# Two-layer hybrid encoder: layer B's output projection as two plain blocks of tokens and three pairs of blocks in seven half-size products

## The chip, the cores and the metric

The kernel runs on one core of a Trainium2 chip. The metric is device time in microseconds (us) of one execution. All matrix products are done on TensorE (PE); VectorE (DVE), ScalarE (ACT) and GpSimd (POOL) prepare operands and take results away; SyncE (SP) issues the DMAs in the order in which they stand in its program.

## What is computed

The reference is one step of an encoder with two attention layers over 2,048 prompt tokens and 64 sample tokens, 2,112 in all, with D_MODEL = 1024:

```
y_p = x_p + (op * jax.nn.silu(gp)) @ w_out
...
y_s = x_s + (os_ * jax.nn.silu(gs)) @ w_out
```

`op` and `os_` are the outputs of the attention of a layer (layer A: sliding window, grouped queries; layer B: 16 heads over the own chunk and 8 chunks before it), `gp` and `gs` the gates, and `w_out` is 1024 x 1024. The case is about this last product of layer B: gated attention (1024 features x 2,112 tokens, the DRAM tensor "ogb") times `w_out_b`, plus the residual x, gives the kernel's y.

## The kernel before

**Numbers and layout.** Activations stand feature-major: 128 partitions x 8 groups of features x 2,112 tokens. Every 32-bit operand of layer B's matmuls is split into two fp16 parts, hi and lo. ACT writes hi by a scaled activation, DVE then writes lo = scaled value - hi by a SCALAR_TENSOR_TENSOR. A product of a 128-row slice of features takes three matmuls: weights hi by x hi, weights hi by x lo, weights lo by x hi. One matmul has a 128 x 128 weight tile and 264 columns of tokens (OT = 2,112 / 8).

**Stages.** Layer A's projections and attention run first, then its output projection, then layer B's projections and attention, head pair by head pair (`hp` 0 to 7), then layer B's output projection. PE's order is written out by hand. While attention runs, a `Filler` (L1029) fills PE between score and value products with the next stage's matmuls, three at a step (L1039); `goal` (L1950) and `due` (L1920) say how many steps to place after each score product. The last head pair's attention is filled with layer B's output projection in this way. What is left of it runs alone at the end. The instructions of the other engines are put into an order by a scheduler; each engine then executes its own in that order, and waits where an operand or a buffer isn't ready.

**Layer B's output projection before** (`output_jobs(1, half, ..)`, L2010). Two halves of the 1024 output features, one after the other; in each half 8 blocks of 264 tokens; in each block 4 output tiles of 128 features; in each tile 8 groups of input features of three matmuls (L2051 to L2053). So 24 matmuls add up in one of two PSUM banks "pj", then one DVE instruction, the combine (L2057), adds bank x scale to a residual tile "res" that a DMA has loaded (L2016). Of every two output tiles a pair is stored (L2069). That makes 64 combines and 1,536 matmuls.

- `load_act` (L576) fetches a block's x in four DMAs of 264 KB (tag "xraw", XB = 4 buffers, L615) and splits each by ACT (L627) and DVE (L628) into "xx" (XN = 7 buffers). As the halves run one after the other, each block is loaded and split twice: 64 loads, 64 splits.
- `load_weights` (L493) loads a half's weights in eight pieces of 128 x 512 and splits each by ACT (L529) and DVE (L530). A half has its own eight, 16 in all.
- `Background` (L428) holds such splits back and places them by a budget: `drain` (L471), `share` (L485).
- POOL has no work in this stage; during the attention it makes the low parts of the softmax values (L1735) and multiplies outputs by gates (L1495).

In attention the instructions that appear in rows of the prediction are the score matmuls (L1678, L1679), the exponential on ACT (L1694) and the query split on DVE (L1633).

## Time and profile before

| | |
|---|---|
| three runs | 2070.81, 2071.38, 2074.5 us; median 2071.38 us |
| profiled execution | span 2081.5 us (the page gives no other time of it) |
| PE | busy 1994.4 us, 96% of the span |
| DVE, ACT, POOL | 68%, 69%, 54% of the span |
| granted PE clock | 9 (90% or more) in each of 40 slices |
| DMA | mean 206 GB/s; 429.11 MB |

In rows of a timeline the first number is the start in us from the span's start, the second the busy time in us; then engine, line, operation, output<-inputs, shape, and "xN" if N neighbouring instructions are drawn as one. In square brackets stands how long the engine stood idle before it and what released it. A row of windows gives from:to, length, then busy us (instructions) of PE, PE's weight load, DVE, ACT and POOL, the granted clock, the DMA share and GB/s. A row of groups gives the line, engine, operation and shape, the count, the busy us in all, the mean ns of one, and the idle time before with its releaser. A row of DMA issues gives count, KB each and the us from issue to landing.

### The profile page before, as it was taken

Reading aid. Unit: us, or ns where it says so; the run is one execution under the profiler, and the core shown is the slowest. Engines: PE = TensorE matmul, PEld = TensorE weight load, DVE = VectorE, ACT = ScalarE, POOL = GpSimd, SP = SyncE. Lnnn points to the kernel's source line nnn. Section 1 sums busy time; section 2 is a strip of 40 time slices with the busy share of each in tenths; the row PEclk is TensorE's granted clock in tenths of the full one; section 3 lists DMA queues with packets and bytes.
Section 4 is the critical chain, followed back from the end, with each engine's and each line's share of the span. In section 5 each row is a group of like instructions: output and inputs, shape, how many; then the busy total and the mean of one; then the engine's idle time right before and its main releaser. Section 6 shows DMA issues by size and latency. Waiting matters only on the chain.

```text
span 2081.5 us, 40775 instructions
## 1 busy us (share of the span) xinstructions
PE 1994.4 (96%) x12814; PEld 1429.3 (69%) x12814; DVE 1405.7 (68%) x4073; ACT 1439.1 (69%) x3572; POOL 1133.0 (54%) x1529
## 2 busy tenths in 40 slices
PE   7898999999999999989999999999999999999999
PEld 6777788777888999745555555555555555557888
DVE  7666777767667555677767676676766767667542
ACT  6777888777788433367778677787877778687430
POOL 5665565454447445578556565665756656565000
PEclk9999999999999999999999999999999999999999
DMA  8878787899766666789889789797987979678763
GB/s 259 252 209 220 218 213 184 228 232 240 210 159 177 197 215 204 265 227 248 218 184 244 167 200 222 175 238 176 201 221 171 245 163 215 154 155 200 229 198 113
DMA packets 610712, 429.11 MB, mean 206 GB/s; under 512 B 404208, under 2 KB 547968, under 8 KB 610464
## 3 DMA queue, kind: packets, MB, share of 16 engines
q1 hardware_dynamic: 610496, 426.51, 79.9%
q8 instruction: 101, 1.65, 0.3%
q14 instruction: 115, 0.94, 0.1%
HBM read 257.59 MB, written 73.43 MB: 159 GB/s over the span
## 4 chain that ended last, share of the span: by engine, by line
PE 54%; DVE 8%; ACT 6%; DMA 5%; issue 4%; POOL 2%; SPq 1%; ACTq 0%; DVEq 0%; POOLq 0%
PE pj L753 9%; PE pj L755 9%; PE pj L754 9%; PE o L1840 4%; PE pj L2051 4%; PE pj L2053 4%; PE pj L2052 4%; PE sb L1678 2%; PE sb L1679 2%; PE tp L1006 1%; DMA pt<-values 1%; DVE p L1682 1%; DVE wh L540 1%; DMA wraw<-in_w_o_a_dram 1%; POOL xx L635 1%
## 5 line engine op out<-in xcount | busy, mean ns | idle before, releaser
L753 PE MATMUL pj<-wh,xx 128*128 128x512 f16 (+2 forms) x1648 | 642.5, 390 | 22.4 <-DVE pa L847 9.6
L755 PE MATMUL pj<-wh,xx 128*128 128x512 f16 (+2 forms) x1648 | 624.0, 379 | 0.6 <-POOL xx L635 0.6
L1735 POOL TENSOR_TENSOR values<-p,values 128x640 f16<-128x640 f32 (+4 forms) x256 | 327.3, 1279 | 205.5 <-ACT values L1734 199.1
L754 PE MATMUL pj<-wh,xx 128*128 128x512 f16 x1024 | 388.3, 379 | 1.3 <-DVE wh L540 1.3
L1694 ACT ACTIVATE p<-p,nm 128x640 f32<-128x640 f32 (+5 forms) x264 | 199.5, 756 | 180.0 <-DVE nm L1687 141.0
L2051 PE MATMUL pj<-xx,wh 128*128 128x264 f32 (+1 forms) x1024 | 290.5, 284 | 11.2 <-DVE res L2057 4.0
L1682 DVE CUSTOM_DVE_ANT_0 p<-sb,BT 128x640 f32<-128x640 f32 (+5 forms) x272 | 196.5, 722 | 150.2 <-PE sb L1679 129.3
L2052 PE MATMUL pj<-xx,wh 128*128 128x264 f32 (+1 forms) x1024 | 287.6, 281 | 0.0
L635 POOL TENSOR_TENSOR xx<-xraw,xx 128x528 fp32r<-128x528 f32 (+4 forms) x144 | 184.7, 1304 | 100.2 <-ACT xx L634 92.9
L754 PE MATMUL pj<-wl,xx 128*128 128x512 f32 (+1 forms) x624 | 235.4, 377 | 2.4 <-DVE wl L540 2.4
L844 POOL TENSOR_TENSOR f<-f,mhalf 128x4 f32<-128x4 f32 x182 | 186.3, 1024 | 12.2
L755 PEld LDWEIGHTS <-xx 128*128 128x128 f16 x1024 | 100.2, 98 | 123.7 <-issue 1.9
L1342 ACT ACTIVATE p<-p,nm 128x257 f32<-128x257 f32 (+2 forms) x272 | 134.4, 496 | 70.5 <-DVE nm L1331 35.8
L1495 POOL TENSOR_TENSOR o<-gt,o 128x256 f32<-128x256 f32 (+1 forms) x132 | 104.9, 794 | 142.2 <-ACT p L1342 72.0
L1734 ACT CAST values<-p 128x640 f16<-128x640 f32 (+4 forms) x256 | 168.2, 658 | 12.5 <-DMA pt<-values 6.5
L754 PEld LDWEIGHTS <-xx 128*128 128x128 f16 x1024 | 100.3, 98 | 83.5 <-issue 3.6
L753 PEld LDWEIGHTS <-xx 128*128 128x128 f16 x1024 | 100.3, 98 | 82.0 <-ACT sq L822 1.4
L1840 PEld LDWEIGHTS <-values 128*128 128x128 f16 x1344 | 123.3, 98 | 38.8 <-DMA pt<-values 2.7
L753 PEld LDWEIGHTS pj<-wh,xx 128*128 128x128 f32 x624 | 119.7, 192 | 40.3 <-issue 8.1
L2053 PE MATMUL pj<-xx,wl 128*128 128x264 f32 x512 | 145.8, 285 | 0.9 <-DVE wl L533 0.9
L1840 PE MATMUL o<-pt,values 128*128 128x256 f16 (+1 forms) x1344 | 143.7, 255 | 1.7 <-DMA pt<-values 1.3
L2053 PE MATMUL pj<-xx,wh 128*128 128x264 f16 x512 | 141.3, 276 | 1.4 <-DVE wh L530 1.4
(292 smaller groups left out, 4719.8 us busy)
## 6 DMA issues: line engine op xcount, KB each, us to landing
xx<-xsb SPq DMA_DIRECT2D x112, 512.0 KB, 4.3
xx<-xsa SPq DMA_DIRECT2D x88, 512.0 KB, 5.0
xraw<-oga SPq DMA_DIRECT2D x64, 264.0 KB, 3.6
xraw<-ogb SPq DMA_DIRECT2D x64, 264.0 KB, 4.0
xsa<-xx SPq DMA_DIRECT2D x32, 512.0 KB, 4.0
wl<-in_w_in_b_dram SPq DMA_DIRECT2D x64, 256.0 KB, 4.9
wraw<-in_w_in_b_dram SPq DMA_DIRECT2D x56, 256.0 KB, 3.5
xraw<-in_x_dram SPq DMA_DIRECT2D x40, 256.0 KB, 4.6
```

The source lines that it names most:

```text
L635: nc.gpsimd.tensor_tensor(lo, rv, wide(hi), op=ALU.subtract)
L753: nc.tensor.matmul(ps[:n, :C], xh, wh, start=k == 0, stop=False)
L754: nc.tensor.matmul(ps[:n, :C], xh, wl, start=False, stop=False)
L755: nc.tensor.matmul(ps[:n, :C], xl, wh, start=False, stop=k == KC - 1)
L844: nc.gpsimd.tensor_tensor(fv, fv, mhalf[:n, :H], op=ALU.pow)
L1682: mi = nc.vector.tensor_tensor_reduce(out=p[r, :nk], in0=S[r, o : o + nk], in1=b, op0=ALU.add, op1=ALU.min, scale=1.0, scalar=3e38, accum_ ...
L1694: ex = nc.scalar.activation(p[:n, :nk], p[:n, :nk], AF.Exp, scale=-1.0, bias=it.nm[:n, c : c + 1], accum_out=it.sm[:n, c : c + 1],)
L1735: lo = nc.gpsimd.tensor_tensor(two[:, :, 1, :], pv, two[:, :, 0, :], op=ALU.subtract)
L1840: nc.tensor.matmul(it.O[:, h * T + q0 : h * T + q1_], held["VH"][:, kt, h], x, start=kt == kb and not low, stop=kt == tb and low == 1,)
L2051: nc.tensor.matmul(ps[:, :OT], wh, oh, start=k == 0, stop=False)
L2052: nc.tensor.matmul(ps[:, :OT], wh, ol, start=False, stop=False)
L2053: nc.tensor.matmul(ps[:, :OT], wl, oh, start=False, stop=k == KC - 1)
```

## The change

The two `output_jobs(1, ..)` give way to `fast_output_jobs(x1, y)`. The 2,112 tokens are taken as two single blocks of 264 ("spans" 0 and 1), then three pairs of blocks (528 tokens, spans 2 to 4).

A **single block** is computed as before, but for all 1024 output features in one pass: 8 output tiles of 24 matmuls and a combine. Two blocks have 384 matmuls and 16 combines.

A **pair** is computed by Strassen's scheme in Winograd's form, which takes 2 x 2 blocks: the two halves of the input features, the two halves of the output features, the two blocks of tokens. It has four groups, m = 0 to 3, one for each 128 features of an output half. A group takes seven products of half the depth: 4 groups of input features x 3 matmuls = 12 matmuls each. The products alternate between two fixed PSUM banks, whose sums run on from product to product, and after each product a combine (L2284 of the kernel after) adds the bank as it then stands to one quarter of the group's residual tiles ("res" for the upper output half, "more" for the lower). Three pairs have 3 x 4 x 7 x 12 = 1,008 matmuls and 84 combines.

**Operands of a pair.** The seven x operands are the raw quarters 0, 1, 2, 3, with four of them used as they are and three made from differences. POOL makes the differences in place in "xraw" (four subtractions of 128 x 528 a half, L2243); then ACT and DVE split each operand (L2192, L2195). It is done in two halves, e = 0 and 1, as "xraw" has four buffers and four quarters fill them: the loads of e = 1 stand behind the splits of e = 0 that read those buffers. So a pair has 8 loads, 14 splits and 8 subtractions. Each operand is a `Step`; a `drip` runs the next step, `force` runs what a product needs and isn't made. `operand(i + 1)` is called while span i runs, so that a pair's operands are made while the span before it is multiplied. Pair 1 and pair 3 lie in "xx", "ph", "pl", pair 2 in "values", "pt", "xx", tiles that the attention used.

**Weights.** `w_o_b` lies in another order in DRAM. There are 16 plain pieces and 16 mixed ones (sums and differences of pieces, by POOL, L2153, 16 operations of 128 x 512); all 32 are split once (ACT L2130, DVE L2131) and kept to the end. They are prepared by drips from step 8 of the last head pair on: one or two in each `due`, and after combines.

So there are 1,392 matmuls for 1,536, 100 combines for 64, 50 splits of x for 64, 40 loads of x for 64, 32 splits of weights for 16 with 32 loads for 16, and 40 POOL operations more. The scales of the splits change from 8 and WB_ to OO = 2 and WO = 2^12, and "ph" and "pl" hold 4 x 256 numbers for 5 x 256.

```diff
-        for half in range(2):
-            output_jobs(1, half, x1, y)
+        fast_output_jobs(x1, y)
...
+        spans = [(0, 1), (1, 1)] + [(2 + 2 * p, 2) for p in range(3)]
...
+        elif at == 8:
+            while held["chain"]:
+                held["chain"].pop(0)()
+            held["prepare"]()
...
                 if at:
                     bg.share(BL, BP_, KC)
+                    drip(1 + (len(drips["x"]) > 0))
...
+    def drip(n=1):
+        for _ in range(n):
+            for chain in drips.values():
+                if chain:
+                    chain[0].run()
+                    break
...
+    def force(*steps):
+        for x in steps:
+            while x.fn is not None:
+                drips[x.kind][0].run()
...
+            def s1():
+                for b in (2, 3, 0):
+                    raws[b] = raw_w(m, b)
+                return pool(3, 2, 3, ALU.add)
...
+        def split_x(dst, raw, guard):
+            hi, lo = (dst[:, :, q] for q in range(2))
+            r = nc.scalar.activation(hi, raw, AF.Identity, scale=S_OG)
...
+            nc.vector.scalar_tensor_tensor(lo, raw, S_OG, hi, op0=ALU.mult, op1=ALU.subtract)
...
+            def split(y_, k, at, less=()):
+                def part(e):
+                    if k == 0 and e:
+                        fetch_half(e)
...
+                    for o, a, b in less:
+                        nc.gpsimd.tensor_tensor(raws[e, o], raws[e, a], raws[e, b], op=ALU.subtract)
+                    split_x(x.parts[y_][:, 2 * e : 2 * e + 2], raws[e, at], tag in ("ph", "pl") and e == 0)
...
+            todo = [
+                split(0, 0, 0),
+                split(1, 1, 2),
+                split(2, 2, 3),
+                split(6, 3, 3, ((0, 1, 0), (1, 3, 1), (3, 3, 0))),
+                split(3, 4, 0),
+                split(4, 5, 1),
+                split(5, 6, 2, ((2, 2, 3),)),
+            ]
...
+        def product(w, x, xi, acc, start, stop=True):
+            force(w, *x.steps[xi])
+            for k in range(4):
...
+                combine(acc, rv[:, e])
+                if not filler.attending:
+                    drip(2)
...
+            for y_, (acc, wi, xi, start, rv) in enumerate((
+                (a, 0, 0, True, top[:, :OT]), (b, 1, 1, True, top[:, :OT]),
+                (a, 5, 6, False, top[:, OT:]), (b, 4, 3, True, bottom[:, OT:]),
+                (a, 6, 4, False, bottom[:, OT:]), (b, 2, 2, False, top[:, OT:]),
+                (a, 3, 5, False, bottom[:, :OT]),
+            )):
+                yield from product(ws[wi], x, xi, acc, start)
+                combine(acc, rv)
+                if not filler.attending and (y_ % 2 or m == 3):
+                    drip()
+                if wi == 2:
+                    store(xout[:, m, rows], top)
+                    next_res(i, m)
...
+                    if ready(i + 1) and (i or m == 4):
+                        st.x[i + 1] = operand(i + 1)
+                    yield from (group if n == 2 else alone)(i, x, m)
```

How instructions stand on DVE in the part that runs alone: before, in the second half of the output features. A combine (L2057) names its "res" tile and its bank "pj"; a split (L628) names its "xx" tile and the "xraw" buffer that it reads.

```order
L2057 SCALAR_TENSOR_TENSOR res_4986_26423<-pj_4988_26451,scl_90,res_4986_26423 128x264
L628 SCALAR_TENSOR_TENSOR xx_5008_26631<-xraw_5004_26612,scl_90,xx_5008_26631 128x528
L628 SCALAR_TENSOR_TENSOR xx_5024_26762<-xraw_5018_26748,scl_90,xx_5024_26762 128x528
L628 SCALAR_TENSOR_TENSOR xx_5024_26762<-xraw_5019_26750,scl_90,xx_5024_26762 128x528
L2057 SCALAR_TENSOR_TENSOR res_4993_26486<-pj_4994_26488,scl_90,res_4993_26486 128x264
L2057 SCALAR_TENSOR_TENSOR res_4993_26486<-pj_4997_26524,scl_90,res_4993_26486 128x264
L2057 SCALAR_TENSOR_TENSOR res_4998_26551<-pj_4999_26553,scl_90,res_4998_26551 128x264
```

And after, at the end of the first pair's group m = 0 and in m = 1. The combine is L2284, the split of an x operand L2195 (of 128 x 2 x 264), the split of a piece of weights L2131; "pj_4982" and "pj_4983" are the two banks.

```order
L2195 SCALAR_TENSOR_TENSOR xx_4996_26494<-xraw_4985_26287,scl_90,xx_4996_26494 128x2x264
L2284 SCALAR_TENSOR_TENSOR more_4974_26209<-pj_4982_26283,scl_90,more_4974_26209 128x264
L2131 SCALAR_TENSOR_TENSOR wl_5019_26701<-wraw_5016_26690,scl_90,wl_5019_26701 128x512
L2284 SCALAR_TENSOR_TENSOR res_4989_26379<-pj_4983_26284,scl_90,res_4989_26379 128x264
L2195 SCALAR_TENSOR_TENSOR pt_4991_26423<-xraw_4987_26291,scl_90,pt_4991_26423 128x2x264
L2195 SCALAR_TENSOR_TENSOR pt_4993_26459<-xraw_4984_26285,scl_90,pt_4993_26459 128x2x264
L2284 SCALAR_TENSOR_TENSOR res_4989_26379<-pj_4982_26283,scl_90,res_4989_26379 128x264
L2195 SCALAR_TENSOR_TENSOR xx_4999_26542<-xraw_4986_26289,scl_90,xx_4999_26542 128x2x264
L2195 SCALAR_TENSOR_TENSOR values_4988_26319<-xraw_5006_26590,scl_90,values_4988_26319 128x2x264
L2284 SCALAR_TENSOR_TENSOR res_4989_26379<-pj_4983_26284,scl_90,res_4989_26379 128x264
```

Before, two or three splits stand together between combines of 24 matmuls each; after, one or two stand between combines of 12 matmuls each. The buffer "xraw_5006" holds a quarter of the second half of pair 2's x. Its load goes into the room of "xraw_4985" and waits for that buffer's last reader, the split in the first row; its own split is the last but one row, ahead of the combine in the last row. From the first row to the last there are four combines, so four products.

On POOL before, the last instructions are those of the attention (o1 is a gated output, L1495 and L1805; "values" the low parts, L1735), and nothing follows them:

```order
L1495 TENSOR_TENSOR o1_4917_25852<-gt_4916_25850,o1_4917_25852 128x256
L1805 TENSOR_TENSOR o1_4929_25922<-G_4887_25614,o1_4929_25922 128x64
L1719 TENSOR_TENSOR G_4934_25974<-pb_4815_25160,sm_4899_25713 128x128 x2
L1735 TENSOR_TENSOR values_2366_11787<-p_4925_25882,values_2366_11787 128x5x128
L1495 TENSOR_TENSOR o1_4950_26113<-gt_4949_26111,o1_4950_26113 128x256
```

After, POOL goes on through the first pair with the differences of pair 2's quarters (L2243) and the mixed pieces of weights (L2153):

```order
L2243 TENSOR_TENSOR xraw_4984_26285<-xraw_4985_26287,xraw_4984_26285 128x528
L2153 TENSOR_TENSOR wraw_5015_26688<-wraw_5014_26686,wraw_5015_26688 128x512
L2153 TENSOR_TENSOR wraw_5014_26686<-wraw_5016_26690,wraw_5014_26686 128x512
L2243 TENSOR_TENSOR xraw_4985_26287<-xraw_4987_26291,xraw_4985_26287 128x528
L2153 TENSOR_TENSOR wraw_5016_26690<-wraw_5015_26688,wraw_5016_26690 128x512
L2243 TENSOR_TENSOR xraw_4987_26291<-xraw_4987_26291,xraw_4984_26285 128x528
L2243 TENSOR_TENSOR xraw_4986_26289<-xraw_4986_26289,xraw_4987_26291 128x528
```

So a split of pair 2's made operands (L2195 on "xraw_4985", "xraw_4987", "xraw_4986") has a POOL instruction ahead of it in which "xraw" is written in place, and that instruction has POOL's rows above it ahead of it. Until the first of layer B's output matmuls, PE's order is the same in both kernels.

211 lines of the change are left out of this document (198 added, 13 removed).

## The prediction

> **What bounds the kernel now.** I read the page first, then a table of windows over the last 250 us, then PE's gaps there, then DVE's timeline and the chain behind the longest gap.
>
> ```profile
> span 2081.5 us, 40775 instructions
> ...
> PE 1994.4 (96%) x12814; PEld 1429.3 (69%) x12814; DVE 1405.7 (68%) x4073; ACT 1439.1 (69%) x3572; POOL 1133.0 (54%) x1529
> ```
>
> PE is the bound over the whole kernel. The change acts only in the stretch in which layer B's output projection runs, so I look at its two parts: beside the last attention (to 1946) and alone.
>
> ```profile
> 1836.00:1890.00 54.00, 51.47 (x330) 31.09 (x329) 42.31 (x111) 48.00 (x107) 37.32 (x46) 1.00 0.81 170
> ...
> 1946.00:2077.00 131.00, 128.35 (x1142) 111.48 (x1141) 50.92 (x88) 27.60 (x41) 0.00 (x0) 1.00 0.58 176
> ```
>
> Alone, PE works 128.35 of 131 us at a granted clock of 1.00; DVE has 80 us to spare, ACT 103, and POOL does nothing. So a matmul that goes there is paid back in full, as long as nothing else takes PE's place. What one costs shows in the steady end:
>
> ```profile
> 2072.35 0.49 DVE L2057 SCALAR_TENSOR_TENSOR res<-pj,scl,res 128x264 f32<-128x264 f32 x1 [2.21 <-PE pj L2053]
> ...
> 2075.05 0.49 DVE L2057 SCALAR_TENSOR_TENSOR res<-pj,scl,res 128x264 f32<-128x264 f32 x1 [2.21 <-PE pj L2053]
> ...
> 2077.75 0.49 DVE L2057 SCALAR_TENSOR_TENSOR res<-pj,scl,res 128x264 f32<-128x264 f32 x1 [2.21 <-PE pj L2053]
> ```
>
> A combine every 2.70 us, so 24 matmuls take 2.70 us: 112.5 ns each. PE's two longest gaps in the stretch, and DVE around the longer one:
>
> ```profile
> 1888.52 0.29 PE L2053 MATMUL pj<-xx,wh 128*128 128x264 f16 x1 [1.35 <-DVE wh L530]
> ...
> 1953.35 0.27 PE L2051 MATMUL pj<-xx,wh 128*128 128x264 f16 x1 [2.65 <-DVE res L2057]
> ```
>
> ```profile
> 1945.44 0.49 DVE L2057 SCALAR_TENSOR_TENSOR res<-pj,scl,res 128x264 f32<-128x264 f32 x1
> ...
> 1952.12 0.77 DVE L628 SCALAR_TENSOR_TENSOR xx<-xraw,scl,xx 128x528 f16<-128x528 f32 x1 [2.48 <-ACT xx L627]
> 1952.81 0.89 DVE L2057 SCALAR_TENSOR_TENSOR res<-pj,scl,res 128x264 f32<-128x264 f32 x2
> ```
>
> ```profile
> 1945.88 5.46 DMA xraw<-ogb
> ...
> 1951.36 0.74 ACT xx L627
> ```
>
> This is the pattern to keep in mind: a combine stood in DVE's queue behind a split whose x came late (5.46 us of DMA, then ACT, then the split). PE had both banks full and waited 2.65 us for the combine.
>
> **The change part by part.**
>
> *Removed.* 1,536 matmuls become 1,392: 144 x 0.1125 = **-16.2 us**. The 1.35 us gap waits for a half's weights; these are now split ahead once for the whole stage, so it goes. The 2.65 us gap is a plain block's late load; what such a load costs in the new order is counted below, so the old one comes off: **-4.0 us**. Together -20.2.
>
> *Tighter.* A product is 12 x 0.1125 = 1.35 us. A bank is needed again one product after its own ends, so the combine's 0.49 us must be over within 1.35 us: slack is 0.86 at most, and I reckon with 0.55 (an estimate: the ways from PE to DVE and back take a part that no row shows apart); before it was 2.70 - 0.49 = 2.21. Whatever stands on DVE ahead of a combine and waits for more than that stops PE.
>
> *What stands there.* The prices in the stretch that runs alone:
>
> ```profile
> L628 DVE SCALAR_TENSOR_TENSOR xx<-xraw,scl,xx 128x528 f16<-128x528 f32 x48 | 35.4, 766 | 17.6 <-ACT xx L627 17.4
> L627 ACT ACTIVATE xx<-xraw,scl 128x528 f16<-128x528 f32 x47 | 32.5, 728 | 71.6 <-PE pj L2053 62.7 <-DMA xraw<-ogb 8.8
> ...
> L530 DVE SCALAR_TENSOR_TENSOR wh<-wl,scl,wh 128x512 f16<-128x512 f32 x7 | 5.0, 743 | 0.6 <-ACT wh L529 0.6
> L529 ACT ACTIVATE wh<-wl,scl 128x512 f16<-128x512 f32 x5 | 3.3, 710 | 7.1 <-PE pj L2053 7.1
> ```
>
> ```profile
> xraw<-ogb SPq DMA_DIRECT2D x35, 264.0 KB, 4.2
> out_dram<-res SPq DMA_DIRECT2D x24, 264.0 KB, 3.3
> res<-x SPq DMA_DIRECT2D x23, 264.0 KB, 2.9
> ```
>
> A reload of "xraw" that waits for the split before it costs 4.2 + 0.73 + 0.77 = 5.7 us from that split to its own (4.4 if it lands like a residual, in 2.9). From the first row of the new DVE order to its last combine lie four products, 5.4 us, the first of them partly over: the reload of xraw_5006 comes about 0.5 us beyond the slack.
>
> Followed along the order in this way:
> - (a) The passage from plain blocks to pair 1, whose second half of operands is loaded as buffers come free: one reload with three products of cover, 5.7 - 4.05 - 0.55, about 1.0 us (0.3 to 2).
> - (b) Pair 1's groups m = 0 and 1, which carry pair 2's operands: first load 1.0; xraw_5006 0.5; xraw_5007, whose issue waits for POOL's last difference and holds xraw_5008 behind it in SP's order, 1.5; xraw_5009 0.5; four splits behind POOL's in-place differences, which need POOL, ACT and DVE in turn, 0.5 each. In all 5.5 us (3.5 to 7.5).
> - (c) From pair 1's m = 3 into pair 2's m = 0, pair 3's operands: two reloads 0.5 each, one behind POOL 1.3: 2.3 us (1 to 3.5).
>
> Pair 2's m = 1 to 3 and all of pair 3 have no split left: 49 products at PE's own pace. The residuals are loaded a group ahead, over 7 x 1.35 = 9.5 us against 2.9, and cost nothing; if that cover went, the first combine of a group would wait the 2.9. SP issues fewer DMAs of x (40 for 64) and 16 more of weights; DMA is busy 0.58 of that stretch. The end after the last matmul (combine, store) stays.
>
> (d) **POOL and DVE.** POOL is idle in this stretch before; now it has 40 instructions, about 21 of them in pair 1 and pair 2's m = 0. A price from the page, and what happens to a split of DVE that meets a POOL instruction:
>
> ```profile
> L635 POOL TENSOR_TENSOR xx<-xraw,xx 128x528 fp32r<-128x528 f32 (+4 forms) x144 | 184.7, 1304 | 100.2 <-ACT xx L634 92.9
> ```
>
> ```profile
> 1859.45 1.48 DVE L530 SCALAR_TENSOR_TENSOR wh<-wl,scl,wh 128x512 f16<-128x512 f32 x1
> ...
> 1858.99 1.40 POOL L1735 TENSOR_TENSOR values<-p,values 128x640 f16<-128x640 f32 x1
> ...
> 1872.26 1.69 DVE L628 SCALAR_TENSOR_TENSOR xx<-xraw,scl,xx 128x528 f16<-128x528 f32 x1
> ...
> 1890.31 1.95 DVE L628 SCALAR_TENSOR_TENSOR xx<-xraw,scl,xx 128x528 f16<-128x528 f32 x1
> ...
> 1890.29 1.40 POOL L1735 TENSOR_TENSOR values<-p,values 128x640 f16<-128x640 f32 x1
> ...
> 1901.99 0.47 DVE L2057 SCALAR_TENSOR_TENSOR res<-pj,scl,res 128x264 f32<-128x264 f32 x1
> ...
> 1901.94 0.73 POOL L1495 TENSOR_TENSOR o<-gt,o 128x256 f32<-128x256 f32 x1 [0.45 <-ACT p L1694]
> ```
>
> The splits took 1.48, 1.69 and 1.95 us where 0.74 and 0.77 are usual: 0.74, 0.92 and 1.18 longer, 0.95 in the mean. They end some 0.5 us after the POOL instruction. The combine beside POOL took its 0.47. The Trainium skill ("SBUF — State Buffer", section "Who interferes with whom") says why: a DVE instruction with two SBUF inputs contends with a GpSimd instruction that reads SBUF, and the loser blocks fully; one with at most one SBUF input doesn't. The trace agrees: the split reads two SBUF tiles, the combine one and PSUM. By that rule each POOL instruction of the change could cost DVE up to its own length.
>
> What it costs here: 35 products take 47.3 us of PE. DVE has in them 35 combines of 0.49 and 34 splits of 0.77: 43.3 us, so 4.0 are free. With a wait of w per POOL instruction it is 43.3 + 21w. How all splits of that time fared (ns: least, median, most), beside a POOL that was busy 37.32 of 54 us:
>
> ```profile
> L628 DVE SCALAR_TENSOR_TENSOR xx<-xraw,scl,xx x4: 755/823/1686, 1872.3 to 1875.4; 128x528 f16<-128x528 f32 x4
> ```
>
> ```profile
> L530 DVE SCALAR_TENSOR_TENSOR wh<-wl,scl,wh x8: 742/956/1482, 1850.9 to 1887.2; 128x512 f16<-128x512 f32 x8
> ```
>
> The median lost 0.06 and 0.21. I take w = 1/3, between these and 0.95: a made operand's split is released by its own POOL instruction's end, and POOL then often waits for DVE. That gives 43.3 + 7.0 - 47.3 = **3.0 us** (0 to 16).
>
> (e) In the last attention six more splits than before stand ahead of the first combine (18 for 12): ACT gets 6 x 0.71 and DVE 6 x 0.74, about 4.3 us each, where ACT is busy 48.00 of 54 us and so sets the pace of some score products. Most falls in its idle 6; I take 1.0 us (0 to 4).
>
> *Sum.* -16.2 - 4.0 + 1.0 + 5.5 + 2.3 + 3.0 + 1.0 = **-7.4 us**. The profiled span goes from 2081.5 to 2074.1. It is 10.1 us above the runs' median; the page gives no other time of it. As the stretch runs at clock 1.00, the microseconds carry over: 2071.4 - 7.4 = **2064.0**.
>
> **The rivals.**
>
> *R1, operands wholly hidden.* If reloads land in 2.9 us or less, 5.7 becomes 4.4, (b) and (c) vanish nearly, and POOL's instructions fall beside combines. Left are (a) and (e): -20.2 + 2 = -18: **2053**. For it: DMA busy is 0.58, and the residuals do land in 2.9. Against it: loads here took 4.2 in the median and 5.46 in the chain.
>
> *R2, DVE becomes the bound.* If every POOL instruction holds a split for the rows' 0.95 us, DVE has 43.3 + 20.0 = 63.3 us for PE's 47.3, so +16.0. As DVE works in order, it fills no wait for a load with anything, and (b) and (c), 7.8, come on top: -20.2 + 16.0 + 7.8 + 1.0 + 1.0 = +5.6: **2077**, slower. The gain is eaten at w = 0.69 (21w = 20.2 - 9.8 + 4.0), and from w = 0.88 on it is slower by over 0.2%. For it: the three stretched splits. Against it: the two medians, beside a POOL that was busier than it will be here (21 x 1.30 = 27 of some 55 us).
>
> *R3, no change.* The terms at their upper ends without DVE as the bound: 2 + 7.5 + 3.5 + 4 + 3 = 20, -20.2 + 20 = 0: **2071**. For it: all chains go through the same four buffers, so a late reload makes the next late. Against it: each stall gives the next reload cover.
>
> That the change doesn't do what it says is excluded: the built program has 144 matmuls fewer on PE.
>
> **How the numbers follow.** About 0.2% (4.1 us) is what a measurement of this kernel can tell from no change. The forecast's case has 0.50, and its own range, 2058 to 2067, is faster throughout. R1 has 0.18, R3 0.16, R2 0.16. So faster 0.68, same 0.16, slower 0.16. The range runs from R1's time to just below R2's, 2053 to 2076, and leaves out half of each, 0.09 + 0.08.
>
> **What would show it.** Right: combines of pair 3 every 1.35 us; PE gaps of 0.5 to 1.5 us with a combine (L2284) as releaser in pair 1 and pair 2's m = 0, 8 to 13 us in all, and behind them splits that wait for ACT and ACT for "xraw<-ogb"; DVE's idle there ended by ACT, not by PE. R1: hardly any gap there. R2: splits of 1.5 us and more all along pair 1, DVE busy nearly all the time. The whole is wrong if the attention's part grows by more than 4 us, if a product of 12 matmuls takes more than 1.40 us without a gap, or if a gap stands in pair 3.

## The result: 11 us slower

| | median | runs | profiled span |
|---|---|---|---|
| before | 2074.31 us (2070.81 to 2080.69) | 8 | 2081.5 us |
| after | 2084.03 us (2081.04 to 2093.23) | 8 | 2086.9 us |

The ratio of after to before is 1.0053 with an interval of 1.0035 to 1.007: 11.0 us slower. (Here and below a ratio becomes microseconds by (ratio - 1) x 2072; a minus is faster than before. Each ratio is against runs of before made beside it.) The forecast was 2064.0 with a range to 2076: wrong in sign and outside the range.

**Where the stage lost its time.** The trace of before reaches the first score product of the last head pair at 1795.3 us, that of after at 1784.8, though the programs don't differ up to there. So I count from that product. From it to the end before takes 286.2 us and after 302.1: 15.9 more in these two traces, 11.0 by the medians.

Part of the loss lies beside the attention. The 120 score products of that head pair take 124.8 us in before and 129.4 in after, with the same matmuls between them. The difference opens between the 40th and the 80th, first in before, then in after, with PE's two largest gaps in or near it (in brackets the idle time and what ended it):

```profile
1837.60:1873.80 36.20, 36.20 (x226) 21.40 (x225) 27.26 (x73) 30.69 (x68) 25.30 (x31) 1.00 0.81 172
```

```profile
1827.10:1867.40 40.30, 36.87 (x226) 21.22 (x225) 33.97 (x79) 33.94 (x75) 27.16 (x31) 1.00 0.91 185
```

```profile
1859.19 0.32 PE L1683 MATMUL sb<-KA,q 128*128 128x384 f16 x1 [1.92 <-DVE nm L1687]
...
1876.58 0.32 PE L1683 MATMUL sb<-KA,q 128*128 128x384 f16 x1 [2.07 <-ACT ws L2130]
```

In before PE is never idle there; in after it is for 3.4 us. DVE does ten splits of the stage's operands in that stretch, where before does five.

Then the stretch that runs alone in after, and its two halves. The columns are those of the prediction's windows.

```profile
1937.00:2087.00 150.00, 129.30 (x1077) 107.39 (x1075) 88.92 (x135) 32.15 (x47) 42.16 (x30) 0.96 0.45 137
...
1946.00:2000.00 54.00, 42.67 (x324) 33.50 (x323) 42.71 (x56) 19.86 (x28) 28.19 (x21) 0.91 0.57 165
...
2000.00:2080.00 80.00, 76.13 (x669) 65.35 (x669) 37.95 (x68) 7.13 (x10) 8.35 (x6) 1.00 0.37 116
```

The same stretch of before, from 1937 to its end:

```profile
1937.00:2082.00 145.00, 137.76 (x1223) 119.31 (x1221) 58.45 (x101) 32.94 (x50) 0.99 (x1) 1.00 0.58 175
```

At 1937 after has 146 matmuls fewer left (1077 for 1223): both kernels have come equally far, and the 144 that the change removes, 16.2 us, are all still to be saved. But after has needed 152.2 us from the first score product to this point and before 141.7. So 10.5 us are lost by then, 4.6 during the score products and the rest behind the last of them, around the gap that ends at 1934.16 below. And from here on the stretch takes 150 us for 145. Two things use the gain up and more: PE stands idle for 20.7 us instead of 7.2, and its matmuls, busy 129.30 us, go at 0.120 us each instead of 0.1126, which is 8 us more; the granted clock has fallen to 0.96. Both lie mostly in the first part, 1946 to 2000 (PE busy 42.67 of 54 us, clock 0.91). From 2000 on PE works 76.13 of 80 us at 1.00, as foreseen.

Here are the largest gaps of PE from 1930 on:

```profile
1934.16 0.27 PE L2291 MATMUL pj<-xx,wl 128*128 128x264 f16 x1 [3.42 <-DVE res L2284]
...
1944.47 0.27 PE L2291 MATMUL pj<-xx,ws 128*128 128x264 f16 x1 [1.77 <-DVE more L2284]
...
1950.75 0.29 PE L2291 MATMUL pj<-xx,wx 128*128 128x264 f16 x1 [3.42 <-DVE res L2284]
...
1968.85 0.27 PE L2291 MATMUL pj<-xx,wx 128*128 128x264 f16 x1 [2.85 <-DVE res L2284]
...
2011.11 0.27 PE L2291 MATMUL pj<-xx,wh 128*128 128x264 f16 x1 [1.53 <-DVE res L2284]
```

Each ends with a combine, as in before. DVE's timeline shows what the combine stood behind, and the chain of waits shows why:

```profile
1943.93 0.48 DVE L2284 SCALAR_TENSOR_TENSOR more<-pj,scl,more 128x264 f32<-128x264 f32 x1
1944.34 4.28 DVE L2195 SCALAR_TENSOR_TENSOR xx<-xraw,scl,xx 128x528 f16<-128x528 f32 x3
1948.54 1.75 DVE L2131 SCALAR_TENSOR_TENSOR wl<-wraw,scl,wl 128x512 f16<-128x512 f32 x1
1950.21 0.48 DVE L2284 SCALAR_TENSOR_TENSOR res<-pj,scl,res 128x264 f32<-128x264 f32 x1
...
1956.99 1.02 DVE L2131 SCALAR_TENSOR_TENSOR wl<-wraw,scl,wl 128x512 f16<-128x512 f32 x1 [2.83 <-ACT wl L2130]
```

```profile
1945.09 3.52 DVE xx L2195 x2
1948.62 1.68 DVE wl L2131
1950.32 4.46 DMA wraw<-in_w_o_b_dram
1954.94 1.27 POOL wraw L2153
1956.23 0.73 ACT wl L2130
```

Two causes stand side by side. From 1944.34 to 1950.21, DVE executes four splits one after the other, which take 4.28 + 1.75 us where four of 0.77 would be 3.1. POOL works all that time, and a combine waits behind the splits and PE behind the combine: the second gap of 3.42 us. And from 1950.32 on, when a split has freed one of the three weight buffers, stands a chain that the prediction has no term for: a *weight* piece is loaded (4.46 us), mixed on POOL (1.27), split on ACT (0.73); the DVE split that ends it waits 2.83 us with the next combine behind it. (PE lost only 0.57 us by that wait, as it ran at half speed then.)

### The profile page after: what moved, and what is told of

The parts are those of the page before. It is cut to its first block, busy times and chain, and to the rows that moved or that the text cites. A ratio compares the mean times of both kernels' runs of the same rounds, so it can differ in the third digit from the quotient of the medians.

```text
span 2086.9 us, 40567 instructions
## 1 busy us (share of the span) xinstructions
PE 1987.4 (95%) x12670; PEld 1416.2 (68%) x12670; DVE 1448.5 (69%) x4111; ACT 1440.5 (69%) x3574; POOL 1191.9 (57%) x1569
## 4 chain that ended last, share of the span: by engine, by line
PE 50%; DVE 10%; DMA 8%; ACT 6%; issue 5%; POOL 2%; SPq 1%; ACTq 0%; POOLq 0%; DVEq 0%
PE pj L758 9%; PE pj L760 9%; PE pj L759 9%; PE o L1847 4%; PE sb L1683 2%; PE sb L1684 2%; PE pj L2059 2%; PE pj L2061 2%; PE pj L2060 2%; PE tp L1011 1%; PE pj L2291 1%; PE pj L2294 1%; PE pj L2295 1%; DVE p L1687 1%; DMA q<-q 1%
## 5 line engine op out<-in xcount | busy, mean ns | idle before, releaser
L849 POOL TENSOR_TENSOR f<-f,mhalf 128x4 f32<-128x4 f32 x182 | 186.3, 1024 | 12.2
L2059 PE MATMUL pj<-xx,wh 128*128 128x264 f32 x512 | 148.5, 290 | 4.3 <-DVE res L2069 1.8
L2060 PE MATMUL pj<-xx,wh 128*128 128x264 f32 x512 | 145.7, 285 | 0.0
L758 PEld LDWEIGHTS pj<-wh,xx 128*128 128x128 f32 x624 | 119.2, 191 | 36.9 <-ACT pa L781 8.2
L760 PEld LDWEIGHTS pj<-wh,xx 128*128 128x128 f32 x624 | 119.0, 191 | 23.1
```

The source lines that it names most:

```text
L758: nc.tensor.matmul(ps[:n, :C], xh, wh, start=k == 0, stop=False)
L760: nc.tensor.matmul(ps[:n, :C], xl, wh, start=False, stop=k == KC - 1)
L849: nc.gpsimd.tensor_tensor(fv, fv, mhalf[:n, :H], op=ALU.pow)
L2059: nc.tensor.matmul(ps[:, :OT], wh, oh, start=k == 0, stop=False)
L2060: nc.tensor.matmul(ps[:, :OT], wh, ol, start=False, stop=False)
```

## The theories and the experiments

- **Theory A** (the prediction's R2): POOL's 40 new instructions hold the two-input splits of DVE, and combines queue behind them.
- **Theory B**: late reloads of x through the four "xraw" buffers, terms (a) to (c).
- **Theory C**: the order on DVE; the splits are put ahead of combines that are more urgent.

Theory D, that the mixed weights' way through three "wraw" buffers is a cost of its own, came up when A to C had been tried.

### A taken away, whole and by halves

e1 leaves all 40 POOL instructions out, so mixed operands are plain pieces; loads and splits stay.

```diff
-                nc.gpsimd.tensor_tensor(raws[dst], raws[x], raws[y_], op=op)
...
-                    for o, a, b in less:
-                        nc.gpsimd.tensor_tensor(raws[e, o], raws[e, a], raws[e, b], op=ALU.subtract)
```

> All 40 POOL instructions of the new output projection are left out (differences of x and mixed weights are not formed; every load, split, combine and matmul stays). Theory A, POOL holds DVE's splits: the splits go back to 0.77 us (1.11 in the kernel after), PE's idle and slow time after the last attention product, 25.8 us in the kernel after, falls to 10 or less, and the kernel is 14 to 20 us faster than the kernel after, so 3 to 9 us faster than before. Theory B, late reloads of the four x buffers: the splits still come late, at most 5 us better. Theory C, splits put ahead of combines in DVE's order whatever holds them: about half, 8 to 12 us.

Measured: 0.9998 (0.9982 to 1.0013), -0.4 us. Without POOL's work the 11 us are gone, less than the 14 to 20 that theory A alone was expected to give, and the gain of 20 isn't there either. e5 leaves out only the 16 weight mixes (the first deletion), e6 only the 24 differences of x (the second).

> Only the 16 POOL instructions that mix weights are left out (the mixed weights are then unmixed ones); the 24 for x stay. All 40 together were worth 11 us. If what they cost is the hold on DVE, each counts alike: 16 of 40, 4 to 5 us faster than the kernel after, and the gaps behind weights (L2131) shrink. If it is the chain load, POOL, ACT, DVE of the weights through three buffers, that is the longer one, and this takes 7 us or more.

> Only the 24 POOL instructions for the differences of x are left out. Hold on DVE: 24 of 40, 6 to 7 us faster than the kernel after. Chain of the weights: 4 us or less.

Measured: e5 1.0017 (1.0002 to 1.0032), +3.5; e6 1.0028 (1.0018 to 1.0039), +5.8. So 16 instructions on weights are worth 7.5 us, 24 on x 5.2: together 12.7, about the 11.4 of e1. Both halves count. The weights' seem to count for more each, but the two intervals overlap. 7.5 us is what was expected of a longer chain of the weights, and 5.2 lies between the two expectations, so these runs don't tell hold from chain.

What the hold is, by the groups of the instructions of a form in 1800 to 2040. First after, then e1 (line, operation, count, busy us, mean ns, idle time before):

```profile
L2195 DVE SCALAR_TENSOR_TENSOR xx<-xraw,scl,xx 128x528 f16<-128x528 f32 x32 | 33.9, 1076 | 5.1 <-ACT xx L2192 4.9
...
L2131 DVE SCALAR_TENSOR_TENSOR wl<-wraw,scl,wl 128x512 f16<-128x512 f32 x12 | 14.4, 1203 | 4.9 <-ACT wl L2130 4.9
...
L2195 DVE SCALAR_TENSOR_TENSOR ph<-xraw,scl,ph 128x528 f16<-128x528 f32 x4 | 5.9, 1476 | 2.0 <-ACT ph L2192 2.0
```

```profile
L2194 DVE SCALAR_TENSOR_TENSOR xx<-xraw,scl,xx 128x528 f16<-128x528 f32 x32 | 25.9, 835 | 3.6 <-ACT xx L2191 3.3
...
L2131 DVE SCALAR_TENSOR_TENSOR wl<-wraw,scl,wl 128x512 f16<-128x512 f32 x12 | 11.0, 940 | 2.3 <-ACT wl L2130 2.3
...
L2194 DVE SCALAR_TENSOR_TENSOR ph<-xraw,scl,ph 128x528 f16<-128x528 f32 x4 | 3.0, 762 | 1.6 <-ACT ph L2191 1.6
```

These three groups lose 8.0, 3.4 and 2.9 us. Over all nine groups (50 splits of x, 32 of weights) it is 92.5 us with POOL and 74.1 without: 18.4 us for 40 POOL instructions, **w = 0.46 us** each.

e4 puts the 40 instructions on DVE instead (both `nc.gpsimd.tensor_tensor` become `nc.vector.tensor_tensor`).

> The 40 POOL instructions are given to DVE (a difference of 128 x 528 some 0.6 to 0.8 us there). Theory A: the splits go back to 0.77 us; DVE gets 40 x 0.7 = 28 us of work and loses some 15 us of waits, so the time is between 5 us better and 10 us worse than the kernel after. If POOL did not hold DVE, it would be 15 us or more worse.

Measured: 1.0052 (1.0038 to 1.0066), +10.8, as after. There they take DVE 17.3 us for x and 12.1 for weights, by these groups of e4:

```profile
L2243 DVE TENSOR_TENSOR xraw<-xraw,xraw 128x528 f32<-128x528 f32 x24 | 17.3, 722 | 1.2 <-DMA xraw<-ogb 1.2
...
L2153 DVE TENSOR_TENSOR wraw<-wraw,wraw 128x512 f32<-128x512 f32 x16 | 12.1, 754 | 5.6 <-DMA wraw<-in_w_o_b_dram 5.5
```

29.4 us of DVE's own work comes out no better than 18.4 us of being held.

### Hold, or only a longer chain?

POOL's instruction is also a link between a load and its split. e7 puts a fill in the place of each (0.5 us, writing the same tile, reading nothing; operands are constants); e9 puts three fills (1.6 us), as long a link as the subtraction.

```diff
-                nc.gpsimd.tensor_tensor(raws[dst], raws[x], raws[y_], op=op)
+                for z in (1.0, 0.5, 1.0):      # e9; e7 has one
+                    nc.gpsimd.memset(raws[dst], z)
```

> Each of the 40 POOL instructions is replaced by one that fills the same tile with a constant: POOL still works in the same places and the splits still wait for it, but it reads nothing. Theory A1, the hold on DVE's second SBUF input: the splits go back to 0.77 us and the time to that without POOL, a ratio to before of 0.998 to 1.002. Theory A2, the added link in the chain of each operand: the ratio stays at 1.004 or above; between the two if the fill is much shorter than the 1.45 us of a subtraction.

> Three fills in a row in the place of each of the 40 POOL instructions, some 1.6 us together: the link through POOL is as long as with the subtractions (1.45 us), but POOL reads nothing. With one fill (0.53 us) the ratio to before was 0.9987. Hold on DVE's second SBUF input: splits stay near 0.78 us and the ratio stays under 1.001. Length of the link: the ratio goes back to 1.003 to 1.006 with splits of 0.78 us that come late.

Measured: e7 0.9987 (0.9977 to 0.9997), -2.7; e9 1.0005 (0.9992 to 1.0018), +1.0. Groups of e9 (1870 to 2040):

```profile
L2245 POOL MEMSET xraw<- 128x528 f32 x72 | 37.1, 540 | 24.0 <-DVE xx L2196 12.4 <-DVE res L2286 4.4 <-DMA xraw<-ogb 3.5
L2196 DVE SCALAR_TENSOR_TENSOR xx<-xraw,scl,xx 128x528 f16<-128x528 f32 x28 | 21.5, 788 | 11.6 <-ACT xx L2193 11.5
```

POOL is as busy as in after (37.1 us, against 35.2 for 24 subtractions), but the splits beside it take 788 ns. So of the 11.4 us, 1.4 are the link's length (from -0.4 to +1.0, within the intervals) and about 10 the hold. A fill waits for its own tile's load only and not for a second input's, so some of a subtraction's waiting may be missing in e9 too, and 10 is an upper figure.

e11 keeps all the work and takes the hold away in the stretch after the attention: ACT copies the raw operand into PSUM banks that the attention has left, and DVE's split reads it there, so that it has one SBUF input. The copy is one more link in each operand's chain.

```diff
+            high = raw
+            if not filler.attending:
+                high = copied().rearrange("p (k s) -> p k s", k=2)[:, :, :OT]
+                nc.scalar.copy(high, raw)
...
-            nc.vector.scalar_tensor_tensor(lo, raw, S_OG, hi, op0=ALU.mult, op1=ALU.subtract)
+            nc.vector.scalar_tensor_tensor(lo, high, S_OG, hi, op0=ALU.mult, op1=ALU.subtract)
```

> All work is kept. Once attention is over, ACT first copies the raw operand of each split into PSUM, and DVE's split reads it there: one SBUF input instead of two; POOL's instructions stay as they are, ACT has one instruction of some 0.7 us more for each split. Hold on DVE's second SBUF input: the splits after attention fall from 1.11 us to 0.8 and the time falls by 5 to 9 us against the kernel after (a ratio to before of 1.001 to 1.003); ACT's copy lengthens each operand's chain by 0.7. If splits were long for another reason: no gain or a loss of some us.

Measured: 1.0027 (1.0013 to 1.0041), +5.6: half the loss is back. Its groups in 1870 to 2040 (the split reads "raw" in PSUM after the attention, "xraw" in SBUF before):

```profile
L2257 POOL TENSOR_TENSOR xraw<-xraw,xraw 128x528 f32<-128x528 f32 x24 | 31.8, 1323 | 22.2 <-ACT raw L2205 9.8 <-DMA xraw<-ogb 9.6 <-DVE o L1499 1.8
L2205 ACT COPY raw<-xraw 128x528 f32<-128x528 f32 x32 | 18.5, 591 | 3.7 <-POOL xraw L2257 3.7
...
L2209 DVE SCALAR_TENSOR_TENSOR xx<-raw,scl,xx 128x528 f16<-128x528 f32 x16 | 11.9, 764 | 6.1 <-ACT xx L2206 3.8 <-ACT raw L2205 2.3
...
L2209 DVE SCALAR_TENSOR_TENSOR xx<-xraw,scl,xx 128x528 f16<-128x528 f32 x12 | 10.7, 920 | 4.7 <-ACT xx L2206 4.6
```

POOL's 24 differences are all still made, and the splits out of PSUM take 764 ns, those out of SBUF, in the attention, 920. Theory A holds: 5.4 us come back with all the work kept, and e9 puts the hold at up to about 10. It can't be the whole: e1, with no POOL at all, misses 20 us of gain.

### B and C by themselves

e2 leaves out the loads of a pair's second half (the first half's raw operands, already changed, stand in). e3 puts each split behind the last combine that is written ahead of it.

```diff
-                        fetch_half(e)
+                        raws.update({(1, q): raws[0, q] for q in range(4)})
```

```diff
+            if "combined" in held:
+                behind(r.ins, held["combined"])
```

> The second half of a pair's x is not loaded; its operands are split from the buffers of the first half (12 loads fewer, the POOL instructions and splits stay). Theory B: 10 us or more faster than the kernel after, most gaps gone. Theory A: 2 to 4 us, since POOL still holds the splits. Theory C: 3 to 6 us.

> The same work; each split of x or weights is only put behind the combine that was written last before it, so that DVE's order is the order in which the program was written, one or two splits between combines all along a pair, none hoisted. Theory C: 8 to 15 us faster than the kernel after. Theory A: the number of POOL instructions that meet a split is the same, but they are spread over 28 products for some 14 to 20: 4 to 8 us faster. Theory B: 5 us, as reloads get more cover.

Measured: e2 1.0066 (1.0048 to 1.0084), +13.7; e3 1.0065 (1.005 to 1.008), +13.5. Neither gains. Reloads of x, the prediction's main term, don't set the time as the kernel stands. In e3 the gaps behind a combine are 2.11 us at most, but now PE waits longest for the weights themselves:

```profile
1977.44 0.29 PE L2299 MATMUL pj<-xx,wl 128*128 128x264 f16 x1 [3.52 <-ACT wl L2130]
...
1994.80 0.29 PE L2299 MATMUL pj<-xx,wl 128*128 128x264 f16 x1 [3.97 <-ACT wl L2130]
```

With the order in PE's favour the operand is late instead: the place of the wait moved, its cause didn't. That pointed to theory D.

### Theory D: the mixed weights

e10 leaves out POOL's work and the mixed weights altogether (plain pieces stand in, without loads and splits). e15 leaves out POOL's work and only the mixed weights' 16 loads; their splits are done, from a piece that is already there.

```diff
-                mixed(m)
+                for i, b in ((4, 0), (6, 1), (5, 2), (2, 3)):      # e10
+                    st.s[m, i] = st.w[m, b]
```

```diff
-                for b in (2, 3, 0):
-                    raws[b] = raw_w(m, b)
+                raws.update({b: held["piece"] for b in range(4)})      # e15
```

> The 16 mixed weights are not made (no loads, no POOL, no splits for them; plain pieces stand in) and the differences of x are left out too, so no POOL instruction is left; x is loaded and split as in the kernel after. Without POOL alone the ratio to before was 0.9998. If the rest of the loss is the mixed weights' 16 loads and splits among the combines: 8 us or more better, a ratio of 0.995 to 0.996. If it is pair 1's and pair 2's operands of x: 0.998 to 1.000.

> No POOL instruction, and the mixed weights' 16 loads are left out: their 16 splits take a piece that is there already, so ACT's and DVE's work for them stays. Without POOL the ratio to before was 0.9998, without POOL, mixed loads and mixed splits 0.9938. If the 12 us between them are waits for loads, with combines behind the waiting splits: 0.994 to 0.996. If they are the splits' own work on ACT and DVE: 0.998 to 1.000.

Measured: e10 0.9938 (0.9919 to 0.9958), -12.8; e15 0.9958 (0.9944 to 0.9973), -8.7. Set beside e1 and after, this is a ladder:

| kernel | us against before | step |
|---|---|---|
| by matmuls and old gaps alone (the prediction's sum, not a run) | -20.2 | |
| e10: no POOL, no mixed weights | -12.8 | 7.4: operands of x, weights' plain pieces, the attention |
| e15: + their splits | -8.7 | 4.1: the splits' own work (the two intervals overlap) |
| e1: + their loads | -0.4 | 8.3: waiting for these loads and their buffers |
| after: + POOL | +11.0 | 11.4: the hold (5.4 by e11, up to about 10 by e9) and the link |

A ladder taken in another order would cut the parts elsewhere, as waits overlap. And the division between splits and loads rests on the medians alone: in the single traces, counted from the first score product of the last head pair, e10, e15 and e1 take 276.1, 284.0 and 286.6 us, 10.5 from first to last where the ladder has 12.4, but 7.9 for the splits and 2.6 for the loads.

### Would more time help?

The weights must be ready when pair 1 begins. e8 takes four plain blocks first and two pairs, so that drips have more products to lie beside; 48 matmuls, 5.4 us, come back. e12 does this on e11.

```diff
-        spans = [(0, 1), (1, 1)] + [(2 + 2 * p, 2) for p in range(3)]
+        spans = [(j, 1) for j in range(4)] + [(4 + 2 * p, 2) for p in range(2)]
```

> Four plain blocks first, then two pairs: 96 matmuls saved for 144 (10.8 us for 16.2), 16 POOL instructions for x for 24, and 16 combines of 2.70 us more in which weights are mixed and pair 1's operands made. If the loss is too little time for preparing before the first pair (all theories): the time lost beside matmuls in the stage, 32 us after against 6 before, falls below 12, and the kernel is 0 to 5 us faster than before. If pairs lose by themselves, each about a third of what three lose: still 3 to 6 us slower than before.

> As the run before, with four plain blocks ahead of two pairs. With four plain blocks alone the ratio was 1.0057, no better than with two. Hold on DVE: the plain blocks' two splits per combine fit again (0.49 + 2 x 0.8 of 2.70 us), the loss beside matmuls falls from 26 us to under 15, and the ratio is 0.998 to 1.002. Otherwise 1.004 or more.

Measured: e8 1.0057 (1.0043 to 1.0071), +11.8; e12 1.0052 (1.0034 to 1.007), +10.8. Beside e11's +5.6, e12 pays its 5.4 us of matmuls and gets nothing for them. Why more time is no use stands in DVE's timeline of e12:

```profile
1948.70 0.75 DVE L2138 SCALAR_TENSOR_TENSOR wl<-raw,scl,wl 128x512 f16<-128x512 f32 x1 [3.75 <-ACT wl L2137]
1949.37 0.48 DVE L2298 SCALAR_TENSOR_TENSOR more<-pj,scl,more 128x264 f32<-128x264 f32 x1
...
1953.12 0.75 DVE L2138 SCALAR_TENSOR_TENSOR wl<-raw,scl,wl 128x512 f16<-128x512 f32 x1 [3.27 <-ACT wl L2137]
```

A drip issues load, ACT and DVE split *together*. The load takes 4 us, the split stands in DVE's queue at once, and in these rows each weight drip stops DVE for 3 to 4 us with a combine behind it, however many products are still to come.

### Loads ahead of splits

e16 is e12 with the drip cut in two: a weight piece's load and POOL instruction are issued two drips ahead of its split (for x, one), splits stand behind the last combine, x and weights take turns, the third x operand goes ahead of the second, a pair's second half is loaded a step earlier, and every second set of mixed pieces has other buffers. e17 is the same with the change's three pairs and a drip after every product. All the work of the change is kept.

```diff
+                    if not filler.attending:
+                        for nxt in chain[: 2 if chain is drips["w"] else 1]:
+                            nxt.begin()
...
+        def begin(self):
+            pre, self.pre = self.pre, None
+            if pre is not None:
+                bg.run(bg.put(0.0, pre, True, True))
```

> All work is kept, four plain blocks and two pairs, raw operands of splits in PSUM (1.0052 so far). New: the load and POOL instruction of a weight piece are issued two drips ahead of its split and those of an x operand one drip ahead, splits stand behind the combine that was written before them, drips of x and weights alternate, every second set of mixed pieces goes to other buffers. If combines lose their time behind splits that wait for loads: the loss beside matmuls falls from 25 us to 12 or less, a ratio of 0.995 to 0.999, faster than before. If the work itself is the loss: 1.003 or more.

> The same pacing with the change's own three pairs and a drip after every product (1.0027 without pacing). 26 to 30 splits then stand among pair 1's 28 products. Waits for loads as the loss: 0.996 to 1.001. Too little time between the attention's end and pair 1: 1.002 or more, with PE itself waiting for weights.

Measured: e16 0.9994 (0.9979 to 1.0008), -1.2; e17 1.0007 (0.9995 to 1.002), +1.5. That is 12.0 us better than e12 and 4.1 better than e11, for edits of order and buffers alone. (A first build of each, e13 and e14, counted its drips with a name that the attention already used for something else; the attention grew by some 460 us, 1.2235 and 1.2206, and they tell nothing.) Windows of e16 and its two largest gaps:

```profile
1937.00:2066.00 129.00, 121.34 (x1075) 104.86 (x1072) 62.08 (x112) 43.13 (x70) 25.92 (x20) 1.00 0.46 141
```

```profile
1925.11 0.30 PE L2333 MATMUL pj<-xx,wl 128*128 128x264 f16 x1 [2.80 <-DVE res L2324]
...
1988.50 0.27 PE L2333 MATMUL pj<-xx,wh 128*128 128x264 f16 x1 [2.44 <-DVE res L2324]
```

From 1937 on PE idles 7.7 us, where after had 20.7 and before 7.2, and its clock is 1.00 again. By the prediction's terms e16 should now be at -(96 x 0.1125 + 4.0) = -14.8; it is at -1.2. As the lone stretch has hardly more idle time than before's, most of these 13.6 us must lie ahead of 1937, beside the attention and at its end. e18 puts the splits behind the last combine there too:

```diff
-            if not filler.attending:
+            if "combined" in held:
                 behind(r.ins, held["combined"])
```

> The paced kernel with four plain blocks (0.9994), with the splits put behind the combine that was written before them during the last attention as well. Two gaps of 2.08 and 2.80 us stand there, behind splits that the scheduler put ahead of a score's maximum and of a combine. If order alone makes them: 2 to 4 us faster, a ratio of 0.9975 to 0.9985, clear of 1. If POOL's hold makes them (in attention the splits still read two SBUF tiles): no change, 0.999 to 1.000.

Measured: 0.9988 (0.9976 to 0.9999), -2.5 us: the fastest version that does all of the work, though not clearly faster than e16, barely faster than before, and 13.5 us faster than after. Its gaps:

```profile
1871.53 0.32 PE L1683 MATMUL sb<-KA,q 128*128 128x384 f16 x1 [2.07 <-ACT ws L2156]
...
1933.62 0.29 PE L2337 MATMUL pj<-xx,ws 128*128 128x264 f16 x1 [2.73 <-DVE more L2328]
...
1987.26 0.27 PE L2337 MATMUL pj<-xx,wh 128*128 128x264 f16 x1 [2.44 <-DVE res L2328]
```

A score matmul waits behind a weight split on ACT (2.07 us). The same gap stands in after, e10 and e16 (2.07, 2.07 and 2.08 us), so POOL's new work doesn't make it. It is absent in e3, but there the score products take 129.8 us all the same. In e16 and e18 the 120 score products take 129.0 and 129.3 us where before takes 124.8, and in e10 127.6: no version of the new stage has them at before's time. Which engine sets it there isn't settled by these runs.

## Why the prediction was wrong

**Right.** The saving in matmuls: behind the last score product 1,225 are left where before has 1,369, and in the end a product takes 1.35 us, one combine after the other:

```profile
2080.61 0.49 DVE L2284 SCALAR_TENSOR_TENSOR more<-pj,scl,more 128x264 f32<-128x264 f32 x1 [0.86 <-PE pj L2295]
2081.96 0.49 DVE L2284 SCALAR_TENSOR_TENSOR res<-pj,scl,res 128x264 f32<-128x264 f32 x1 [0.86 <-PE pj L2295]
```

No gap stands in pair 3, no residual was waited for, and the mechanism of the losses (a combine in DVE's queue behind a split that isn't ready, PE behind the combine) was the one named. Of the prediction's own signs that the whole is wrong two came up: the attention's part grew by 4.6 us, more than the 4 it allowed, and products took more than 1.40 us without a gap where the clock was 0.50. It went wrong in what was counted to stand there. The forecast lost 12.8 of the 20.2 us; measured are 31.2.

- **The step that failed: "What stands there" follows the reloads of x, and weights were priced at nothing.** The 16 mixed pieces need loads through three buffers, 4.0 us each in the median, a POOL instruction and two splits, all at the time at which pair 1 needs them. The prediction counts splits only as busy time of DVE in (d), which leaves 4.0 us free, and the 16 loads only as DMA traffic; no term is a wait for them. Measured: 4.1 + 8.3 = 12.4 us, by e10, e15 and e1; the sum is clear, its two parts less so. The forecast's own row of weight splits in before (L530, idle before it 0.6 us) stands among its prices, but it is a row of only seven such splits.
- **(d), POOL's hold, was too small.** The sign of the term and its mechanism were right; w was taken as 0.33 and is 0.46, on all 40 instructions rather than 21. Terms (b) and (c) held another 3.8 us for links behind POOL (0.5 x 4, and by my estimate 1.0 for xraw_5007's issue and 0.8 of the 1.3), so POOL had 6.8 us in the sum. Measured: 11.4. The right w alone would have given (d) 43.3 + 21 x 0.46 - 47.3 = 5.7: the term asks whether DVE has time enough in all, but a combine is late as soon as the splits just ahead of it are. The medians of before misled: they count splits that met no POOL instruction, whereas a made operand's split can come when POOL makes the next one.
- **(a), (b), (c), (e) without POOL: 6.0 forecast, 7.4 measured** (e10). The size was right in sum, but by luck in part. (e) was 1.0 (0 to 4) and is too small: in e10's trace the score products take 2.8 us longer than in before's, though before's gap of 1.35 us, which lies among them, is gone. That is some 4 us, in after some 6. Of the 7.4 this leaves some 3 for the others, which had 5.0; their single parts weren't measured, and e2 shows no gain from leaving half of a pair's loads out. What (e) missed is when the splits come: ten instead of five between the 40th and the 80th score product, in e10 as in after. That they make the 4 us is read from the trace; no run moves them.
- **The clock was taken as 1.00.** It was 0.96 over the last 150 us, so some 6 to 8 of the 31.2 us are PE at half speed after gaps; they are contained in the parts above, since each was measured with the gaps that it caused.

12.4 + 4.6 + 1.4 = 18.4 is what the forecast missed, from -7.4 to +11.0. R2 named the right sign and the right queue, but its price (w = 0.95) was too high, and it had no weights either; that it came near in time (+5.6 against +11.0) is partly two errors that cancel. The 40 loads of x that the forecast and the text before it name are 32, four for each single block and eight for each pair; no term was worked out from the 40.

**Open.** In e16 and e18 some 12 to 14 us of the forecast's saving are still missing. In e16's trace about 5.5 of them lie among the score products (4.2 us longer than in before, and before's gap of 1.35, counted as gained) and about 7.5 behind the last one (155.5 us, where before has 161.4, the matmuls take off 10.8 and the old gap 2.65), some of that around the gap of 2.80 us at 1925.11, ahead of the lone stretch; whether ACT, DMA or the DVE order sets the time there was not separated. One candidate was not tried at all: SP issues loads in its order, so a load stands behind a store or a residual that waits. In e12 the weight load at 1949.52 was issued only when a store that began at 1944.30 had landed and the residual behind it was issued. A wider "wraw" was tried only for every second set, together with the new order, so the share of buffers and of order in e16's 12 us isn't known.

## What to carry to other kernels

When a change replaces matmuls by operand work, list every operand that the new order makes, its weights too, and follow each from DMA issue to split with the engines' in-order queues in mind: on DVE a split that waited 3 to 4 us for a load (e12) stopped everything behind it, however idle DVE was on average. Issue loads some steps ahead of the instruction that consumes them, and keep that instruction behind the work that PE waits for; more time between steps (e8, e12) or the order alone (e3) gained nothing here, and earlier loads alone were not run. A change that puts operand work beside an earlier stage has to be priced there too. A POOL instruction beside two-input DVE splits is to be priced with its hold on those that are released near it, not with the median of all.

## What the hardware showed that was not expected

**PE's clock was halved after some gaps of 1.5 to 3.4 us.** The gap of 3.42 us in after ended at 1950.75; from 1952.0 to 1958.6 the granted clock was 0.50. Windows of that time:

```profile
1952.00:1953.00 1.00, 0.41 (x3) 0.13 (x1) 1.00 (x3) 0.22 (x1) 0.00 (x0) 0.50 0.81 174
...
1954.00:1956.00 2.00, 2.00 (x11) 1.39 (x10) 0.16 (x1) 0.00 (x0) 1.06 (x1) 0.50 0.91 246
...
1958.00:1959.00 1.00, 0.57 (x3) 0.23 (x2) 1.00 (x3) 0.23 (x1) 0.23 (x1) 0.58 0.50 60
```

In 2.00 us PE starts 11 matmuls, where it starts about 18 at 0.1125 us each. In e10 a gap of 2.31 us sufficed; the clock was low behind it from about 1939.4 to 1942.7. That gap, and the window, and then one of after, behind the gap of 2.07 us that ended at 1876.58:

```profile
1938.66 0.27 PE L2290 MATMUL pj<-xx,wl 128*128 128x264 f16 x1 [2.31 <-DVE res L2283]
```

```profile
1940.00:1942.00 2.00, 2.00 (x11) 1.37 (x9) 2.00 (x5) 1.36 (x2) 0.00 (x0) 0.50 0.91 295
```

```profile
1878.00:1880.00 2.00, 2.00 (x6) 0.73 (x5) 1.74 (x7) 1.98 (x5) 1.85 (x3) 0.50 0.94 289
```

The gaps of 2.08 and 2.44 us in e16 and that of 2.65 us in before (1953.35) had no such stretch behind them, but the gap of 2.44 in e18 (1987.26) had one, with the clock at 0.59 and 0.56 in 1988 to 1992. e16's window behind its 2.44:

```profile
1988.00:1990.00 2.00, 1.50 (x14) 1.31 (x14) 1.61 (x4) 0.70 (x2) 1.30 (x1) 1.00 1.04 343
```

In e8 the clock was 0.50 from 1896 to 1898, and the longest gap just ahead was one of 1.51 us (ended 1894.33). So a gap of 1.5 to 3.4 us may cost nothing more, or half of the 3.3 us or 6.6 us that PE then runs at half speed; the length of the gap alone doesn't tell which. The Trainium skill ("TensorE: Matmul & The Clock Gate", section "HAM oscillation — how this bites in real kernels") gives the rule "no PE-idle gaps >~3.4µs". These runs show that shorter gaps can do it too.

**A write-only POOL instruction didn't hold the splits, and a PSUM input freed them.** The fills of e9 left the splits at 788 ns (800 in the same window of e1, without any of the stage's POOL instructions), and reading the raw operand from PSUM left them at 764 ns while POOL made its differences. POOL gained as well: its subtraction takes 1.32 us in e11 and 1.47 in after, where it is:

```profile
L2243 POOL TENSOR_TENSOR xraw<-xraw,xraw 128x528 f32<-128x528 f32 x24 | 35.2, 1468 | 27.7 <-DVE xx L2195 12.7 <-DVE wl L2131 4.1 <-DMA xraw<-ogb 3.9
```

The Trainium skill ("SBUF — State Buffer", section "Who interferes with whom") says that such a split contends with a GpSimd instruction that reads SBUF and not with one that only writes it; the trace agrees, with these numbers.
